# Paired 64-row scores, stacked parts for the banded heads, and grouped matmuls in a two-network kernel on Trainium2

## The chip, the cores and the metric

One Trainium2 chip (trn2), one core of it. The metric is the device time of one execution in microseconds, the median of the runs shown. TensorE (PE) does all matmuls and transposes, PEld are its weight loads; VectorE (DVE), ScalarE (ACT) and GpSimd (POOL) do the elementwise work, SP issues all DMAs.

## The reference, cut to what matters

Two small networks in a row, each of two layers, on 512 tokens of width 1024, all in float32. Every layer is a mixer (attention and other branches), in the first network also attention to a memory, and a gated feed-forward network. The attention parts that the change touches:

```python
# first network, both layers: 12 heads of 64 in 3 groups of dilation (1, 4, 16), causal
sc = jnp.einsum("bhqd,bhqkd->bhqk", qb[g], kk) * scale      # masked outside the window
o = softmax(sc) @ vv                                        # groups merged by their log sums
# second network, layer 0, "A": 8 banded heads over 2 key heads, band of 128, 256 context keys, a sink
p_loc, p_ctx, _ = joint_softmax(s_loc, s_ctx, s_sink)
# second network, layer 0, "B": 4 heads with two maps each, 512 + 256 keys
o = (softmax(q1 @ k1) - lam * softmax(q2 @ k2)) @ v
# second network, layer 1: latent attention, 16 heads of 64 + 32, 512 + 256 keys
```

## The kernel before, in words

Tokens stand in four tiles of 128 (two more for the 256 context tokens). Weights come from memory in units of up to 128 x 1024 (`wload`, line 124): SP loads `raw` (three buffers), ScalarE writes the high part `whi` (line 109), VectorE the low part `wlo` (line 112), five buffers of each. A product of two such split operands takes three matmuls: high by high, high by low, low by high (`mm3`, lines 134 to 138). Scores and projections are done that way; transposes, the products of probabilities with values and the small dilated scores are plain float32.

The attention of a mixer is a list of items, one per query tile and head, each with four steps: `qk` (scores into the PSUM tile S, two buffers of two banks, and the row minimum of the negated scores on VectorE), `soft` (exponential on ScalarE, scaling on GpSimd), `tr` (transposes through the PSUM tile T, copied back by ScalarE and VectorE as PT), `pv` (products with the values into p). `pipeline` (line 382) records the steps of different items interleaved, and after each turn some further work out of a list (`fill`): the next projection, the convolution or the pooling branch, in steps that each tell a length in ns.

Heads are 64 wide, so scores use 64 rows of the array: head or map 0 has partitions 0 to 63, head 1 has 64 to 127 (`rows` in `items1`, `diff_items`, `window_items`). `pv_pair` (line 439) puts two heads into the two column halves in turn. The stretches are the first network's mixer in both layers (`items1`, 32 items), the second network's first mixer (`diff_items`: 32 items and 8 of context; `window_items`: 32 banded items and 8 of context), and its second (`mla_items`, 96 rows, which uses `pv_pair` too).

The order on each engine is not what is written. A framework records the instructions and orders them by its own reckoning of when each could start, allots the buffers and sets semaphores; each engine then runs its list strictly in order. Names in the lists: a semaphore `DVE_49`, `Activation_49`, `Pool_49`, `PE_49` counts what that engine has finished, `DMAHW0_49` to `DMAHW7_49` count landed loads, `PE_sequencer_49` what TensorE's sequencer has passed.

Of the kernel before, what the change touches and what calls it, by code (L numbers as in the profile page):

```python
# [21 lines left out]
P = 128  # L22
S = 512
# [55 lines left out]
class Net:  # L79
# [398 lines left out]
    def items1(self, p, g, fill, oT):  # L478

        mm = self.nc.tensor.matmul  # L480
        sh = {}
        out = []

        def item(b, h):
            st = {}
            rows = slice(64 * h, 64 * h + 64)
            qs = slice(b * P, (b + 1) * P)

            def qk():
                if (b, h) == (0, 0):  # L490
                    fill.need(p)
                q0, k0, q12, k12 = g["q0"], g["k0"], g["q12"], g["k12"]
                ps = self.psum("S")
                self.mm3(ps[:, 0], (q0[rows, 0, qs], q0[rows, 1, qs]), (k0[rows, 0], k0[rows, 1]), True, True)
                for j in range(2):
                    o = ps[:, 1, j * P : (j + 1) * P]
                    mm(o, lhsT=q12[rows, j, qs], rhs=k12[rows, j, qs], start=True, stop=True)
                st["s"] = ps.rearrange("p a b -> p (a b)")[:, :768]
                st["nm"] = self.nmax(st["s"], mask=self.mask1[:, b])

            def soft():
                st["P"], r = self.exps(st["s"], st["nm"], 768)
                self.norm_probs(st["P"], r)

            def tr():
                sh[b, h] = self.probs_T(st["P"], 6)

            def pv():
                v = g["v"]
                o = self.psum("p")[:, :P]  # L510

                def vs(hh, k):
                    c = hh * 64 + (max(k - 3, 0)) * P
                    return v[:, k if k < 4 else b, c : c + 64]

                self.pv_pair(o, [sh[b, 0], sh[b, 1]], vs)
                self.copy(oT[:, qs], o)

            return (qk, soft, tr, pv if h else None)

        return [item(b, h) for b in range(4) for h in range(2)]
# [506 lines left out]

    def proj_ab(self, hT, i, g, tags, tiles=(0, 1, 2, 3, 4, 5)):
# [14 lines left out]
        lst = [("a", tok, 0, sc), ("b", tok, P, 1.0 if i < 4 else sc)] + ([("c", v, 0, 1.0)] if i == 4 else [])  # L1044
        for n, src, col, s in lst:
            g[n] = self.qk.tile([P, 2, 768], R, name="qk")
            yield from self.transposed(src, col, (4, 5), g[n], s, tag=tags[0])
            yield from self.transposed(src, col, range(4), g[n], s, tag=tags[-1])
        g["v"] = v

    def diff_items(self, h, g, fill, oB):
# [20 lines left out]
        def item(t, m, first):  # L1072
            st = {}
            rows = slice(64 * m, 64 * m + 64)
            q = slice(t * P, (t + 1) * P)

            def qk():
                if first:
                    fill.need(h)
                qT, kT = g["a"], g["b"]  # L1080
                ql = (qT[rows, 0, q], qT[rows, 1, q])
# [3 lines left out]
                st["s"] = ps.rearrange("p a b -> p (a b)")[:, :768]  # L1085
                st["nm"] = self.nmax(st["s"])

            def soft():
                sh.setdefault(t, []).append(self.exps(st["s"], st["nm"], 768))
                if m:  # L1090
                    combine(t)
# [4 lines left out]
            return (qk, soft, tr if m else None, (lambda: finish(t, 6)) if m else None)  # L1096

        def ctx_item(t):
            st = {}
            q = slice(t * P, (t + 1) * P)  # L1100

            def qk():
                qT, kT = g["a"], g["b"]
                ps = self.psum("S")
                st["nm"] = nm = self.sm.tile([P, 2], F32, name="nm2")
                for m in range(2):
                    rows = slice(64 * m, 64 * m + 64)
                    self.mm3(ps[:, m, :256], (qT[rows, 0, q], qT[rows, 1, q]), (kT[rows, 0, 512:], kT[rows, 1, 512:]), True, True)
                nc.vector.tensor_reduce(nm, ps[:, :, :256], axis=AX.X, op=ALU.min)
                st["s"] = ps  # L1110

            def soft():
                sh[t] = [self.exps(st["s"][:, m, :256], st["nm"][:, m : m + 1], 256) for m in range(2)]
                combine(t)

            def tr():
                sh["T", t] = self.probs_T(sh[t][0][0], 2)

            return (qk, soft, tr, lambda: finish(t, 2))

        return [item(t, m, t == 0 and m == 0) for t in range(4) for m in range(2)] + [ctx_item(t) for t in (4, 5)]
# [11 lines left out]
    def window_items(self, g4, g5, fill, oB, oT):  # L1133
# [3 lines left out]

        def item(t, c, kv):
            st = {}
            rows = slice(64 * kv, 64 * kv + 64)  # L1140
# [6 lines left out]
            def qk():  # L1147
                qT, kT = qs(c), g4["c"]
                ql = (qT[rows, 0, q], qT[rows, 1, q])
                ps = self.psum("S")  # L1150
                c0 = 512 - nl * P
                self.mm3(ps[:, 0, c0:], ql, (kT[rows, 0, k0 * P : k1 * P], kT[rows, 1, k0 * P : k1 * P]), True, True)
                self.mm3(ps[:, 1, :256], ql, (kT[rows, 0, 512:], kT[rows, 1, 512:]), True, True)
# [21 lines left out]
        def ctx_item(t, half, kv):  # L1175
            st = {}
            rows = slice(64 * kv, 64 * kv + 64)
            q = slice(t * P, (t + 1) * P)

            def qk():  # L1180
                kT = g4["c"]
                ps = self.psum("S")
                st["s"] = ps[:, 0].rearrange("p (c k) -> p c k", c=2)
                for c in range(2):
                    qT = qs(2 * half + c)
                    self.mm3(st["s"][:, c], (qT[rows, 0, q], qT[rows, 1, q]), (kT[rows, 0, 512:], kT[rows, 1, 512:]), True, True)
# [41 lines left out]
    def mix_ab(self, hT, lead):  # L1228
        nc, I = self.nc, self.I
        with ExitStack() as ctx:  # L1230
            with ExitStack() as c2:
# [25 lines left out]
                for i in range(1, 6):  # L1257
                    fill.add(i, self.proj_ab(hT, i, gs[i], ("p",)))
                items = []
                for h in range(4):  # L1260
                    items += self.diff_items(h, gs[h], fill, oB[h])
                n, oT = len(items), []
                items += self.window_items(gs[4], gs[5], fill, oB, oT)
                self.pipeline(items, fill, [3000] * n + [200] * (len(items) - n), (0, 1, 4, 5))
# [447 lines left out]
```

## Time and profile before

| | |
|---|---|
| median of 3 runs | 3590.36 us (3587.81 to 3595.63) |
| the profiled execution | 3594.31 us |
| its span, first to last instruction | 3592.5 us |
| TensorE busy | 3519.9 us, 98% |
| mean granted TensorE clock | 0.994 of full speed |

The profile is of one execution. Matmul durations overlap, since a matmul streams in while the one before it drains: what a matmul costs is the distance between starts. "x2" behind a row is two instructions merged. Plain float32 matmuls show as two records each.

### The profile page before, as it was taken

What the parts mean: (1) busy time and instruction counts of PE and PEld (TensorE: products, weight loads), DVE (VectorE), ACT (ScalarE), POOL (GpSimd) and SP (SyncE); (2) the same over time, 40 slices, a digit from 0 to 9 for tenths busy, and PEclk for the clock granted to TensorE, in tenths of its full rate; (3) what the DMA queues carried; (4) which work ended last, traced back from release to release, by engine and by line L of the source; (5) the groups of instructions that cost most, each with busy time, mean ns of one, the idle gap of its engine ahead of it and who ended that gap; (6) DMA issues with size and microseconds to landing.
All of it is one profiled execution on the core that took longest, in us unless ns stands there. A gap on an engine that the chain in (4) does not pass through costs nothing.

```text
span 3592.5 us, 48260 instructions
## 1 busy us (share of the span) xinstructions
PE 3519.9 (98%) x19261; PEld 2994.1 (83%) x19261; DVE 1917.2 (53%) x3018; ACT 1335.5 (37%) x2372; POOL 429.1 (12%) x572
## 2 busy tenths in 40 slices
PE   8999999999999999999999999999999989999998
PEld 8877798888898778888878887888888878888887
DVE  4453357466534335666766666536663466753243
ACT  4432344332443324532344446332111356643222
POOL 0211111000102111200011122200000122220001
PEclk9999999999999999999999999999999999999999
DMA  4233334344322433354431112335443121022232
GB/s 129 83 129 94 100 112 141 106 144 135 103 66 93 135 94 124 121 167 150 131 107 40 36 48 77 125 93 168 132 132 103 46 80 33 25 89 87 90 102 86
DMA packets 110130, 364.02 MB, mean 101 GB/s; under 512 B 16617, under 2 KB 18209, under 8 KB 109905
## 3 DMA queue, kind: packets, MB, share of 16 engines
q1 hardware_dynamic: 109904, 360.94, 31.7%
q8 instruction: 151, 2.47, 0.3%
q14 instruction: 75, 0.61, 0.1%
HBM read 347.16 MB, written 13.73 MB: 100 GB/s over the span
## 4 chain that ended last, share of the span: by engine, by line
PE 90%; DVE 3%; ACT 2%; POOL 2%; DMA 1%; issue 1%; SPq 0%; ACTq 0%; POOLq 0%; DVEq 0%
PE ps L136 21%; PE ps L137 21%; PE ps L138 21%; PE p L136 4%; PE p L137 4%; PE p L138 4%; PE T L430 3%; PE p L444 3%; PE S L136 2%; PE S L137 1%; PE S L138 1%; DMA adaw<-in_ada_w_dram 1%; PE T L138 1%; PE T L136 1%; PE T L137 1%
## 5 line engine op out<-in xcount | busy, mean ns | idle before, releaser
L112 DVE TENSOR_TENSOR wlo<-raw,whi 128x1024 fp32r<-128x1024 f32 (+2 forms) x510 | 603.8, 1190 | 734.6 <-ACT whi L109 719.3
L109 ACT ACTIVATE whi<-raw 128x1024 fp32r<-128x1024 f32 (+2 forms) x510 | 518.1, 1019 | 1113.1 <-PE ps L137 710.2
L137 PE MATMUL ps<-hTlo,whi 128*128 128x512 f32 (+1 forms) x2048 | 757.6, 370 | 4.1 <-DVE hTlo L177 4.0
L136 PE MATMUL ps<-hThi,whi 128*128 128x512 f32 (+1 forms) x2048 | 757.7, 371 | 2.7 <-ACT hThi L109 1.4
L138 PE MATMUL ps<-hThi,wlo 128*128 128x512 f32 (+1 forms) x2048 | 756.7, 370 | 0.0
L136 PEld LDWEIGHTS ps<-hThi,whi 128*128 128x128 f32 x2048 | 385.8, 189 | 73.0 <-issue 3.5
L137 PEld LDWEIGHTS ps<-hTlo,whi 128*128 128x128 f32 x2048 | 386.5, 189 | 69.9 <-DVE hTlo L177 4.5
L138 PEld LDWEIGHTS ps<-hThi,wlo 128*128 128x128 f32 x2048 | 386.3, 189 | 65.2
L930 DVE SCALAR_TENSOR_TENSOR acc<-adaw,cs,acc 128x1024 f32<-128x1024 f32 x168 | 209.4, 1279 | 14.6 <-DMA adaw<-in_ada_w_dram 14.3
L136 PE MATMUL ps<-whi,a 128*128 128x512 f32 x440 | 170.9, 392 | 0.7 <-ACT a L109 0.7
L138 PE MATMUL ps<-whi,a 128*128 128x512 f32 x440 | 170.6, 390 | 0.0
L137 PE MATMUL ps<-wlo,a 128*128 128x512 f32 x440 | 170.6, 390 | 0.0
L136 PE MATMUL p<-whi,hThi 128*128 128x384 f32 x464 | 163.1, 352 | 7.5 <-ACT hThi L175 3.1
L137 PE MATMUL p<-wlo,hThi 128*128 128x384 f32 x464 | 158.2, 341 | 4.7 <-DVE wlo L112 4.7
L154 POOL TENSOR_SCALAR rstd<-ms 128x1 f32<-128x1 f32 x78 | 24.1, 309 | 1137.9 <-ACT junk L152 1122.7
L138 PE MATMUL p<-whi,hTlo 128*128 128x384 f32 x464 | 158.2, 341 | 0.7 <-DVE hTlo L112 0.7
L262 DVE TENSOR_TENSOR y<-y,ps 128x1024 f32<-128x1024 f32 x88 | 106.6, 1218 | 85.7 <-PE ps L138 85.4
L136 PE MATMUL ps<-whi,act 128*128 128x512 f32 x352 | 138.2, 395 | 0.0
L137 PE MATMUL ps<-wlo,act 128*128 128x512 f32 x352 | 137.2, 392 | 0.0
L138 PE MATMUL ps<-whi,act 128*128 128x512 f32 x352 | 136.3, 390 | 0.0
L420 POOL TENSOR_SCALAR g<-g,den 128x768 f32<-128x768 f32 (+3 forms) x88 | 74.6, 850 | 424.3 <-DVE den L416 375.6
L109 ACT ACTIVATE PT<-T 128x384 f32<-128x384 f32 (+2 forms) x160 | 74.4, 465 | 111.6 <-PE T L430 109.6
(407 smaller groups left out, 6830.8 us busy)
## 6 DMA issues: line engine op xcount, KB each, us to landing
raw<-in_ffn_w_dram SPq DMA_DIRECT2D x132, 512.0 KB
adaw<-in_ada_w_dram SPq DMA_DIRECT2D x96, 512.0 KB
raw<-in_w_up_dram SPq DMA_DIRECT2D x88, 512.0 KB
raw<-in_w_gate_dram SPq DMA_DIRECT2D x48, 512.0 KB
raw<-in_w_down_dram SPq DMA_DIRECT2D x44, 512.0 KB
raw<-in_w_qkv_dram SPq DMA_DIRECT2D x48, 384.0 KB
xd<-x SPq DMA_DIRECT2D x20, 512.0 KB
raw<-in_w_conv_dram SPq DMA_DIRECT2D x18, 512.0 KB
```

The source lines that it names most:

```text
L109: return self.nc.scalar.activation(out, in_, AF.Copy, scale=scale)
L112: return self.nc.vector.tensor_tensor(out, a, b, op=ALU.subtract)
L136: mm(ps, lhsT=l[0], rhs=r[0], start=first, stop=False)
L137: mm(ps, lhsT=l[0], rhs=r[1], start=False, stop=False)
L138: mm(ps, lhsT=l[1], rhs=r[0], start=False, stop=last)
L154: nc.gpsimd.tensor_scalar(r, ms, 1.0, EPS, op0=ALU.mult, op1=ALU.add)
L262: self.nc.vector.tensor_tensor(yps[t], yps[t], y, op=ALU.add)
L420: self.nc.gpsimd.tensor_scalar(Pt, Pt, r, 1.0, op0=ALU.mult, op1=ALU.mult)
L430: nc.tensor.transpose(ps[:, k * P : (k + 1) * P], Pt[:, (k0 + k) * P : (k0 + k + 1) * P], self.ident)
L444: self.nc.tensor.matmul(o[64 * h : 64 * h + 64], lhsT=vs(h, k), rhs=PTs[h][:, k], start=k == 0, stop=k == nk - 1)
L930: nc.vector.scalar_tensor_tensor(acc[r], w, c, acc[r], op0=ALU.mult, op1=ALU.add)
```

## The change

Scores of two heads (or two maps) are one item now, with both S buffers: `mm3_two` issues each of the three products for head 0 and head 1 in turn. For the banded heads, `stacked` puts the high part of the queries on a head's own 64 partitions and the low part on the other 64, and `keys_twice` puts the same keys on both; two matmuls of 128 rows then give the three products and the low by low one. The grouped scores, and all products with the values, stand in `tc.tile_critical()`, which makes a group one unit for the framework's order. The turns (`steps`), the fill lengths and the order of the fill work differ too.

```diff
+    def mm3_two(self, pss, ls, rs):
+
+        for i, j in ((0, 0), (0, 1), (1, 0)):
+            for ps, l, r in zip(pss, ls, rs):
+                self.nc.tensor.matmul(ps, lhsT=l[i], rhs=r[j], start=(i, j) == (0, 0), stop=i == 1)
...
     def pipeline(self, items, fill, ns, steps=(0, 1, 2, 3)):
-        for i in range(len(items) + steps[-1]):
+
+        own = [it[4] if len(it) > 4 else steps for it in items]
+        for i in range(max(j + o[3] for j, o in enumerate(own)) + 1):
             for s in (0, 2, 1, 3):
-                j = i - steps[s]
-                if 0 <= j < len(items) and items[j][s] is not None:
-                    items[j][s]()
+                for j, it in enumerate(items):
+                    if j + own[j][s] == i and it[s] is not None:
+                        it[s]()
...
     def pv_pair(self, o, PTs, vs):
 
         nk = PTs[0].shape[1]
-        for k in range(nk):
-            for h in range(2):
-                self.nc.tensor.matmul(o[64 * h : 64 * h + 64], lhsT=vs(h, k), rhs=PTs[h][:, k], start=k == 0, stop=k == nk - 1)
+        with self.tc.tile_critical():
+            for k in range(nk):
+                for h in range(2):
+                    self.nc.tensor.matmul(o[64 * h : 64 * h + 64], lhsT=vs(h, k), rhs=PTs[h][:, k], start=k == 0, stop=k == nk - 1)
...
-    def items1(self, p, g, fill, oT):
+    def items1(self, p, g, proj, oT):
...
             def qk():
-                if (b, h) == (0, 0):
-                    fill.need(p)
+                if b == 0 and p:
+                    drain(proj)
                 q0, k0, q12, k12 = g["q0"], g["k0"], g["q12"], g["k12"]
-                ps = self.psum("S")
-                self.mm3(ps[:, 0], (q0[rows, 0, qs], q0[rows, 1, qs]), (k0[rows, 0], k0[rows, 1]), True, True)
-                for j in range(2):
-                    o = ps[:, 1, j * P : (j + 1) * P]
-                    mm(o, lhsT=q12[rows, j, qs], rhs=k12[rows, j, qs], start=True, stop=True)
-                st["s"] = ps.rearrange("p a b -> p (a b)")[:, :768]
-                st["nm"] = self.nmax(st["s"], mask=self.mask1[:, b])
+                pss = [self.psum("S") for _ in both]
+                with self.tc.tile_critical():
+                    self.mm3_two([ps[:, 0] for ps in pss], [(q0[r, 0, qs], q0[r, 1, qs]) for r in both], [(k0[r, 0], k0[r, 1]) for r in both])
+                    for j in range(2):
+                        for ps, r in zip(pss, both):
+                            mm(ps[:, 1, j * P : (j + 1) * P], lhsT=q12[r, j, qs], rhs=k12[r, j, qs], start=True, stop=True)
+                st["s"] = [ps.rearrange("p a b -> p (a b)")[:, :768] for ps in pss]
+                st["nm"] = [self.nmax(s, mask=self.mask1[:, b]) for s in st["s"]]
...
-                fill.add(1, self.proj1(l, 1, hT, gs[1], ("p",)))
+                proj = self.proj1(l, 1, hT, gs[1], ("p",))
+                fill.add("conv", self.conv_branch(l, hT, bF))
                 fill.add("pool", self.pool_in(l, hT, pooled))
-                fill.add("conv", self.conv_branch(l, hT, bF))
                 fill.add("pool", self.pool_out(l, pooled, aF))
-                self.pipeline(self.items1(0, gs[0], fill, oF[0]) + self.items1(1, gs[1], fill, oF[1]), fill, 7200, (0, 1, 2, 3))
+                items = self.items1(0, gs[0], None, oF[0]) + self.items1(1, gs[1], proj, oF[1])
+                self.pipeline(items, fill, [9000] * 4 + [8500] * 4, (0, 0, 1, 2))
...
+    def stacked(self, tok, col, tiles, dst, scale, tag):
...
+        for h in range(2):
+            own, other = slice(64 * h, 64 * h + 64), slice(64 - 64 * h, 128 - 64 * h)
+            self.copy(dst[own, h, c], ps[own], scale=scale)
+            self.nc.vector.scalar_tensor_tensor(dst[other, h, c], ps[own], scale, f32(dst[own, h, c]), op0=ALU.mult, op1=ALU.subtract)
...
+    def keys_twice(self, g):
...
+            for kv, k in enumerate(ks):
+                own, other = slice(64 * kv, 64 * kv + 64), slice(64 - 64 * kv, 128 - 64 * kv)
+                self.split(k[own, 0, c], k[own, 1, c], ps[own])
+                self.copy(k[other, 0, c], ps[own])
+                self.sub(k[other, 1, c], ps[own], f32(k[own, 0, c]))
...
-                ps = self.psum("S")
-                self.mm3(ps[:, 0], ql, (kT[rows, 0, :512], kT[rows, 1, :512]), True, True)
-                self.mm3(ps[:, 1, :256], ql, (kT[rows, 0, 512:], kT[rows, 1, 512:]), True, True)
...
+                with self.tc.tile_critical():
+                    for j, c, n in ((0, slice(0, 512), 512), (1, slice(512, 768), 256)):
+                        self.mm3_two([ps[:, j, :n] for ps in pss], ql, [(kT[r, 0, c], kT[r, 1, c]) for r in both])
...
+        def scores(ps, c, kv, q, keys):
+
+            k = g4["k", kv]
+            for i in range(2):
+                self.nc.tensor.matmul(ps, lhsT=qs(c)[:, kv, q], rhs=k[:, i, keys], start=i == 0, stop=i == 1)
```

TensorE's list at the first scores of the first network. Before:

```order
L137 MATMUL p<-wlo,hThi 128x384
L138 MATMUL p<-whi,hTlo 128x384
L136 MATMUL S<-qk 128x512
L137 MATMUL S<-qk 128x512
L138 MATMUL S<-qk 128x512
L497 MATMUL S<-qk 128x128 x2
L136 MATMUL p<-whi,hThi 128x384 [waits Activation_49]
```

After the change, at the same place:

```order
L138 MATMUL p<-whi,hTlo 128x384
L503 NO_OP [waits DVE_49,Activation_49]
L136 MATMUL p<-hThi,whi 128x512 [waits Activation_49]
L1761 UNCONDITIONAL_BRANCH [waits DMAHW2_49,DMAHW1_49,DMAHW3_49,DMAHW0_49,DMAHW4_49,PE_sequencer_49,DMAHW5_49,DVE_49,DMAHW6_49,PE_49,DMAHW7_49,Activation_49,Pool_49]
L144 MATMUL S<-qk 128x512 x6
L507 MATMUL S<-qk 128x128 x4
L503 UNCONDITIONAL_BRANCH
L137 MATMUL p<-hTlo,whi 128x512 [waits PE_49]
L503 NO_OP [waits PE_sequencer_49]
L138 MATMUL p<-hThi,wlo 128x512 [waits DVE_49]
```

Both heads' scores (L144, L507) are together now, behind a row that waits for thirteen semaphores, and the convolution's matmuls (L136 to L138 with 512 columns) lie around them where the projection's did.

SP's list of the same mixer, from the projections' weights on. Before:

```order
L129 DMA raw<-in_w_qkv_dram 128x768 x16
L129 DMA raw<-in_w_pool_dram 128x1024 x3
L129 DMA raw<-in_w_conv_dram 128x1024 x9
L129 DMA raw<-in_pool_w_dram 128x896
L129 DMA raw<-in_w_abc_dram 128x1024
```

After the change; each branch row marks where a unit of TensorE's lies in the common order, and itself waits for nothing:

```order
L129 DMA raw<-in_w_qkv_dram 128x768 x4
L129 DMA raw<-in_w_conv_dram 128x1024 x5
L1761 UNCONDITIONAL_BRANCH
L129 DMA raw<-in_w_conv_dram 128x1024 x2
L129 DMA raw<-in_w_qkv_dram 128x768 x2
L1761 UNCONDITIONAL_BRANCH
L129 DMA raw<-in_w_qkv_dram 128x768 x2
L1761 UNCONDITIONAL_BRANCH x2
L129 DMA raw<-in_w_qkv_dram 128x768
L1761 UNCONDITIONAL_BRANCH
```

Seven of the nine loads for the convolution come ahead of the twelve for the second projection, and the units lie between the loads.

TensorE's list in the last mixer, from the transposes of a second head on (L430, L438 the transposes, L444, L453 the products with values). Before:

```order
L430 MATMUL T<-ident,big 128x128 [waits DVE_49]
L430 MATMUL T<-ident,big 128x128 x2
L444 MATMUL p<-PT,v 64x128 x12
L136 MATMUL S<-kThi_23729,hClo 128x512 [waits Activation_49]
L137 MATMUL S<-kTlo_23730,hClo 128x512
```

After the change, at the corresponding place:

```order
L438 MATMUL T<-ident,big 128x128 x2
L450 NO_OP [waits PE_sequencer_49,DVE_49,Activation_49]
L136 MATMUL S<-kThi_23820,hChi 128x512 [waits Activation_49]
L1761 UNCONDITIONAL_BRANCH [waits DMAHW2_49,DMAHW1_49,DMAHW3_49,DMAHW0_49,DMAHW4_49,PE_sequencer_49,DMAHW5_49,DVE_49,DMAHW6_49,PE_49,DMAHW7_49,Activation_49,Pool_49]
L453 MATMUL p<-PT,v 64x128 x12
L450 UNCONDITIONAL_BRANCH
L137 MATMUL S<-kTlo_23821,hChi 128x512 [waits PE_49]
L450 NO_OP [waits PE_sequencer_49]
L138 MATMUL S<-kThi_23820,hChi 128x512
```

The twelve products stood between transposes and scores with no wait of their own; now a wait for all semaphores stands ahead of them, and they lie inside the next head's three score passes. The whole list has 104 such rows: 36 ahead of scores and 68 ahead of products.

## Rows read from the trace of the kernel before

**Rows 1.** Page, part 1: busy time, share of the span, instructions of each engine
```profile
PE 3519.9 (98%) x19261; PEld 2994.1 (83%) x19261; DVE 1917.2 (53%) x3018; ACT 1335.5 (37%) x2372; POOL 429.1 (12%) x572
```

**Rows 2.** Page, part 4: shares of the chain that ended last, by engine
```profile
PE 90%; DVE 3%; ACT 2%; POOL 2%; DMA 1%; issue 1%; SPq 0%; ACTq 0%; POOLq 0%; DVEq 0%
```

**Rows 3.** Stretches: length, busy us of PE, PEld, DVE, ACT, POOL; clock, DMA share, GB/s
```profile
72.80:250.20 177.40, 174.66 (x1023) 148.72 (x1022) 79.79 (x159) 69.55 (x119) 32.13 (x44) 0.99 0.29 92
998.50:1175.50 177.00, 174.55 (x1022) 148.43 (x1021) 78.56 (x158) 69.18 (x116) 31.32 (x40) 0.99 0.28 89
1903.30:2142.00 238.70, 234.08 (x1407) 207.56 (x1408) 151.11 (x378) 99.20 (x257) 41.76 (x75) 1.00 0.13 43
2142.00:2231.00 89.00, 87.78 (x716) 67.97 (x716) 63.78 (x244) 59.63 (x190) 29.52 (x46) 1.00 0.06 16
2949.70:3173.00 223.30, 221.42 (x1896) 194.74 (x1896) 156.60 (x330) 145.34 (x313) 60.03 (x64) 1.00 0.11 33
```

**Rows 4.** Timeline, TensorE, first scores of the kernel: start us, duration us, line
```profile
72.60 0.34 PE L138 MATMUL p<-whi,hTlo 128*128 128x384 f32 x1
72.87 0.50 PE L136 MATMUL S<-qk 64*128 64x512 f32 x1
73.21 0.39 PE L137 MATMUL S<-qk 64*128 64x512 f32 x1
73.44 0.39 PE L138 MATMUL S<-qk 64*128 64x512 f32 x1
73.67 0.60 PE L497 MATMUL S<-qk 64*128 64x128 f32 x4
74.20 0.45 PE L136 MATMUL p<-whi,hThi 128*128 128x384 f32 x1
74.49 0.34 PE L137 MATMUL p<-wlo,hThi 128*128 128x384 f32 x1
74.66 0.33 PE L138 MATMUL p<-whi,hTlo 128*128 128x384 f32 x1
```

**Rows 5.** Timeline, TensorE, two context score groups that met
```profile
2128.66 0.39 PE L136 MATMUL S<-qk 64*128 64x256 f32 x2
2128.89 0.29 PE L137 MATMUL S<-qk 64*128 64x256 f32 x2
2129.01 0.29 PE L138 MATMUL S<-qk 64*128 64x256 f32 x2
2129.14 0.28 PE L136 MATMUL S<-qk 64*128 64x256 f32 x1
2129.26 0.28 PE L137 MATMUL S<-qk 64*128 64x256 f32 x1
```

**Rows 6.** Groups by line: busy us, mean ns of one, idle before and releasers
```profile
L399 DVE TENSOR_REDUCE nm<-S 128x1 f32<-128x768 f32 x96 | 91.4, 952 | 44.3 <-PE S L138 43.8
L411 ACT ACTIVATE g<-S,nm 128x768 f32<-128x768 f32 x64 | 57.7, 901 | 26.1 <-DVE nm L399 17.8 <-DVE nm L401 6.2 <-POOL t L578 1.4
L420 POOL TENSOR_SCALAR g<-g,den 128x768 f32<-128x768 f32 x56 | 54.2, 968 | 354.9 <-DVE den L416 324.7 <-issue 22.1 <-PE p L444 5.5
```

**Rows 7.** Timeline, SP queue and ScalarE, around the same first scores
```profile
71.72 2.41 SPq L129 DMA_DIRECT2D raw<-in_w_qkv_dram  x3
...
74.86 0.85 ACT L109 ACTIVATE whi<-raw 128x768 fp32r<-128x768 f32 x1 [1.39 <-DMA raw<-in_w_qkv_dram]
```

**Rows 8.** Busy time by stretch, two of 6 us ahead of the last mixer; columns as rows 3
```profile
2925.00:2931.00 6.00, 2.75 (x21) 2.23 (x19) 5.01 (x8) 3.79 (x8) 1.34 (x3) 1.00 0.58 186
2931.00:2937.00 6.00, 3.49 (x11) 3.52 (x12) 1.50 (x2) 1.03 (x2) 2.93 (x4) 0.53 0.13 36
```

**Rows 9.** Instructions of line 444: the one semaphore instruction on the TensorE queue
```profile
L444 PEldq EVENT_SEMAPHORE  x1: 51/51/51, 2229.3 to 2229.3; - x1
```

**Rows 10.** Waits of ScalarE: us in total, times, longest
```profile
ACT whi L109 <- PE ps L137: 710.2, 213, 7.1
```

More of the change, by code (lines that the diff above doesn't have):

```diff
@@ L514, in vs @@
                     return v[:, k if k < 4 else b, c : c + 64]
[L516 removed]
+                self.pv_pair(o, sh[b], vs)
                 self.copy(oT[:, qs], o)
[L519 to L521 removed]
+            return (qk, soft, tr, pv)
+        return [item(b) for b in range(4)]
     def shifts(self, dst, src, k):
@@ L1043, in proj_ab, with diff_items @@
         sc = -(64 ** -0.5)
-        lst = [("a", tok, 0, sc), ("b", tok, P, 1.0 if i < 4 else sc)] + ([("c", v, 0, 1.0)] if i == 4 else [])
+        lst = [("a", tok, 0, sc), ("b", tok, P, 1.0 if i < 4 else sc)]
         for n, src, col, s in lst:
             g[n] = self.qk.tile([P, 2, 768], R, name="qk")
-            yield from self.transposed(src, col, (4, 5), g[n], s, tag=tags[0])
-            yield from self.transposed(src, col, range(4), g[n], s, tag=tags[-1])
+            to = self.transposed if i < 4 else self.stacked
+            yield from to(src, col, (4, 5), g[n], s, tag=tags[0])
+            yield from to(src, col, range(4), g[n], s, tag=tags[-1])
         g["v"] = v
-    def diff_items(self, h, g, fill, oB):
+    def keys_twice(self, g):
+        ks = (self.qk.tile([P, 2, 768], R, name="qk"),
+              self.work.tile([P, 6, 256], R, name="tok").rearrange("p a b -> p (a b)").rearrange("p (a b) -> p a b", a=2))
+        for tiles in ((4, 5), range(4)):
+            n = len(tiles) * P
+            yield 0.0
+            ps = self.psum("p")[:, :n]
+            for j, t in enumerate(tiles):
+                self.nc.tensor.transpose(ps[:, j * P : (j + 1) * P], g["v"][:, t], self.ident)
+                yield 109
+            c = slice(tiles[0] * P, tiles[0] * P + n)
+            for kv, k in enumerate(ks):
[3 more added lines that the diff above has]
+                self.sub(k[other, 1, c], ps[own], f32(k[own, 0, c]))
+        g["k", 0], g["k", 1] = ks
+    def diff_items(self, h, g, fill, oB, after):
         nc = self.nc
@@ L1070, in finish, with item, tr @@
             nc.vector.scalar_tensor_tensor(oB[:, t], o, r, self.subln, op0=ALU.mult, op1=ALU.mult)
-        def item(t, m, first):
+        def item(t):
             st = {}
-            rows = slice(64 * m, 64 * m + 64)
+            both = [slice(0, 64), slice(64, 128)]
             q = slice(t * P, (t + 1) * P)
             def qk():
-                if first:
+                if t == 0:
                     fill.need(h)
+                    fill.add(*after)
                 qT, kT = g["a"], g["b"]
-                ql = (qT[rows, 0, q], qT[rows, 1, q])
-                ps = self.psum("S")
-                self.mm3(ps[:, 0], ql, (kT[rows, 0, :512], kT[rows, 1, :512]), True, True)
-                self.mm3(ps[:, 1, :256], ql, (kT[rows, 0, 512:], kT[rows, 1, 512:]), True, True)
-                st["s"] = ps.rearrange("p a b -> p (a b)")[:, :768]
-                st["nm"] = self.nmax(st["s"])
-            def soft():
-                sh.setdefault(t, []).append(self.exps(st["s"], st["nm"], 768))
-                if m:
+                ql = [(qT[r, 0, q], qT[r, 1, q]) for r in both]
+                pss = [self.psum("S") for _ in both]
+                with self.tc.tile_critical():
+                    for j, c, n in ((0, slice(0, 512), 512), (1, slice(512, 768), 256)):
+                        self.mm3_two([ps[:, j, :n] for ps in pss], ql, [(kT[r, 0, c], kT[r, 1, c]) for r in both])
+                st["s"] = [ps.rearrange("p a b -> p (a b)")[:, :768] for ps in pss]
+                st["nm"] = [self.nmax(s) for s in st["s"]]
+            def soft():
+                sh[t] = [self.exps(s, nm, 768) for s, nm in zip(st["s"], st["nm"])]
+                combine(t)
+            def tr():
+                sh["T", t] = self.probs_T(sh[t][0][0], 6)
+            return (qk, soft, tr, lambda: finish(t, 6), (0, 0, 2, 3))
@@ new lines, in ctx_item, with qk, soft @@
+        def ctx_item():
+            st = {}
+            def qk():
+                qT, kT = g["a"], g["b"]
+                both = [slice(0, 64), slice(64, 128)]
+                for t in (4, 5):
+                    st[t] = self.psum("S"), self.sm.tile([P, 2], F32, name="nm2")
+                with self.tc.tile_critical():
+                    for t in (4, 5):
+                        q = slice(t * P, (t + 1) * P)
+                        self.mm3_two([st[t][0][:, m, :256] for m in range(2)], [(qT[r, 0, q], qT[r, 1, q]) for r in both],
+                                     [(kT[r, 0, 512:], kT[r, 1, 512:]) for r in both])
+                for ps, nm in st.values():
+                    nc.vector.tensor_reduce(nm, ps[:, :, :256], axis=AX.X, op=ALU.min)
+            def soft():
+                for t, (ps, nm) in st.items():
+                    sh[t] = [self.exps(ps[:, m, :256], nm[:, m : m + 1], 256) for m in range(2)]
@@ L1091, in soft @@
                     combine(t)
             def tr():
-                sh["T", t] = self.probs_T(sh[t][0][0], 6)
[L1096 to L1119, printed above, removed]
@@ L1121, in diff_items @@
-        return [item(t, m, t == 0 and m == 0) for t in range(4) for m in range(2)] + [ctx_item(t) for t in (4, 5)]
+                for t in st:
+                    sh["T", t] = self.probs_T(sh[t][0][0], 2)
+            return (qk, soft, tr, lambda: [finish(t, 2) for t in st], (0, 0, 2, 3))
+        return [item(t) for t in range(4)] + [ctx_item()]
     def diff_T(self, oB, oT):
@@ L1184, in qk @@
                 for c in range(2):
-                    qT = qs(2 * half + c)
-                    self.mm3(st["s"][:, c], (qT[rows, 0, q], qT[rows, 1, q]), (kT[rows, 0, 512:], kT[rows, 1, 512:]), True, True)
+                    scores(st["s"][:, c], 2 * half + c, kv, q, slice(512, 768))
             def soft():
@@ L1256, in mix_ab, with last @@
                 oB = [oBp.tile([P, 6, P], F32, name=f"oB{h}") for h in range(4)]
-                for i in range(1, 6):
-                    fill.add(i, self.proj_ab(hT, i, gs[i], ("p",)))
+                proj = [(i, self.proj_ab(hT, i, gs[i], ("p",))) for i in range(1, 6)]
                 items = []
                 for h in range(4):
-                    items += self.diff_items(h, gs[h], fill, oB[h])
+                    items += self.diff_items(h, gs[h], fill, oB[h], proj[h])
+                qk5 = items[-1][0]
+                def last():
+                    qk5()
+                    fill.add(*proj[4])
+                    fill.add(5, self.keys_twice(gs[4]))
+                items[-1] = (last,) + items[-1][1:]
                 n, oT = len(items), []
                 items += self.window_items(gs[4], gs[5], fill, oB, oT)
-                self.pipeline(items, fill, [3000] * n + [200] * (len(items) - n), (0, 1, 4, 5))
+                self.pipeline(items, fill, [6000] * 20 + [200] * (len(items) - n), (0, 1, 4, 5))
                 fill.drain()
```

30 lines of the change are left out of this document (18 added, 12 removed).

## The prediction

> **What bounds the kernel now.** First the page's busy shares: TensorE is busy 3519.9 of 3592.5 us [rows 1], so it idles 73 us in all. Second the chain that ended last: 90% of it is TensorE, every other engine 3% or less [rows 2]. Third the stretches in which attention is computed, five of them, 905 us together [rows 3]: in each TensorE is busy 98 to 99% of the time, VectorE 44 to 72%. So a step removed from TensorE's queue there is worth its full length, and a stop put into that queue costs its full length. Fourth the timeline, for what one step costs. Steps are read from start to start, since the durations overlap.
>
> **What the change takes off TensorE.** *Passes.* In [rows 4] a 64-row pass of 512 columns starts 0.23 us after the one before it, and the four short passes of line 497 take 0.60 us with a last one of some 0.27, so 0.11 each. One head of the first mixer is 3 x 0.23 + 4 x 0.11 = 1.13 us. Are two row halves as quick as one? The old order brought three couples together by chance ("x2") [rows 5]: couple follows couple after 0.12 us, and the single passes behind them follow each other after 0.12 us as well. A couple costs what a single costs. So 16 pairs in the first mixer (2 layers, 2 projections, 4 blocks) give 16 x 1.13 = 18 us; 16 pairs of the two-map heads (3 x 0.23 + 3 x 0.12 = 1.05 each) 17 us; their 8 context tiles (3 x 0.12) 3 us. The banded heads go from 3 passes to 2: 32 items save one pass of 256 or 384 columns (0.12, or 0.17 as a projection pass in [rows 4]) and one of 256, 8 us; their context items 8 x 2 x 0.12 = 2 us. Sum 48 us; if 512-column couples did not overlap, 10.
>
> Rule against row: a couple adds about 0.01 us to a single in [rows 5]. The Trainium skill, "TensorE: Matmul & The Clock Gate", Part 3, "Measured speedup vs the span model", gives a four-fold row packing as 3.07 times; the same loss for two tiles would make 38 us of these savings about 26, and the total 12 us later. The couples of [rows 5] are this kernel's own, so I keep 48.
>
> *Changes of shape.* When TensorE goes from 128 to 64 rows in [rows 4], the first 64-row pass starts 0.27 us after the last projection pass in place of 0.17, and the next after 0.34 in place of 0.23; on the way back the projection's first step is 0.29 in place of 0.17. That is 0.2 us for one change, 0.1 if its second half is hidden. The built lists have 452 such changes before and 240 after, because grouped passes are no longer cut by projections and transposes and the banded scores are 128 rows high. 212 x 0.2 = 42 us (21 at least). Together TensorE's own work is 90 us shorter.
>
> **What it adds.** The built order is what I rest on. Each of the 104 grouped units (36 of scores, 68 of products with values, 32 of those in the last mixer, which has no other edit) stands behind a row that waits for thirteen semaphores. They are TensorE's own matmuls, ScalarE, VectorE, GpSimd, and all eight semaphores on which loads land; each value is that of the last instruction or load listed ahead of the unit, needed by it or not. Behind the unit the next matmuls stand behind a wait for TensorE's own semaphore, until it is empty. Nothing in the trace of before is such a stop, so each part of its cost is bounded.
>
> *Emptying.* The last matmul must end: 0.34 us in [rows 4] where the next began after 0.27. One semaphore instruction on TensorE's queue is 0.05 us [rows 9]. Behind the unit the same, and the next weights are not loaded ahead, 0.1 us more. I take 0.3 us for both ends, 31 us in all (bounds 0.15 and 0.6: 16 and 62).
>
> *Loads.* In 33 units the newest load stands at most 15 matmuls ahead, in 21 of them at most 5. Three loads issued from 71.72 let ScalarE go on at 74.86: the first landed 3.1 us after its issue [rows 7]. With 5 or fewer matmuls of 0.17 to 0.23 us gone, about 2.6 us are left, with 10 or so gone 1.1: 21 x 2.6 + 12 x 1.1 = 68 us. Below, nothing is left of it; above, 33 x 3.1 = 102. Until now such a load was covered by the projection's own matmuls; that cover is what the wait removes.
>
> *Other engines.* The other 71 units wait for the last instruction listed on VectorE, ScalarE or GpSimd; in 89 of the 104 one of them stands within 3 matmuls, so it has hardly begun. One is the row minimum at 0.95 us, the exponential at 0.90 or the scaling at 0.97 [rows 6]. I take one whole instruction, 71 x 0.95 = 67 us. Below, a third of one (22); above, minimum and exponential in a row (131).
>
> *Refilling.* While TensorE stands, the others run out of scores and transposes, so the next transposes wait for minimum, exponential and scaling, 2.8 us in a row [rows 6], as far as no projection covers it. Mostly one does: I take 0.3 us a unit, 31 us (0 to 62).
>
> *Clock.* In the 6 us to 2931 TensorE worked 2.75 us, and in the 6 us behind that its granted clock was 0.53, between the two levels 1.2 and 2.4 GHz but nearly the lower [rows 8]. Stops of 3 us may bring that on. Those 6 us lost at most 0.47 x 6 = 2.8 us of TensorE's work; I take half of that for one stop and six such stops, 10 us (0 to 35).
>
> *At no cost.* The stacked parts and doubled keys add 14 instructions each to ScalarE and VectorE, of 0.4 to 0.9 us; they lie in the stretch from 1903 to 2142, where VectorE is busy 151 of 239 us [rows 3]. If that cover failed, about 8 us. The first mixer's second projection is now run in one piece before its first pair, and the convolution branch fills the first half instead: the same matmuls and the same loads in another order on SP's queue, seven of the convolution's ahead of the projection's twelve. Its cost is in the loads above, since a wait on them is what the new order can hit. Queued behind a waiting TensorE are the projections, so all weight buffers are freed later, and SP's next loads with them.
>
> **The sum.** -48 - 42 + 31 + 68 + 67 + 31 + 10 = +117 us. The profiled execution took 3594.3 us, 1.8 around its span and 4 over the median of the runs shown: 3594 + 117 = **3711 us**.
>
> **Rivals.**
> 1. *The waits are met already* (faster). Then only the emptying is paid: 3594 - 90 + 31 = 3535 us. For it: ScalarE's weight splits spend 710 us waiting for TensorE [rows 10], so the others mostly stand ready. Against it: what they wait for is a buffer that TensorE has just freed, so split and load begin just then and are what the next unit must wait for. It decides if loads, engines, refilling and clock cost under 59 us, 0.57 a unit; up to 3590. Chance 0.07.
> 2. *Every wait is a long one.* Loads 102, engines 131, clock 35, the rest as above: 3594 - 90 + 31 + 102 + 131 + 31 + 35 = 3834 us. It needs the landing to be slower than in [rows 7], or two instructions in front of each unit. Chance 0.10.
> 3. *The readers of the scores set the pace.* A pair takes both score buffers, and the next pair waits for two minima and two exponentials, 3.7 us [rows 6]; then the 38 us of the pairs come to nothing: 3749. Against it, groups stand about 12 us apart (239 us for 16 pairs and 4 context groups [rows 3]). The Trainium skill, "TensorEngine Tiling (Array Packing)", "PSUM Bottleneck", says that tiling speeds up TensorE but not the reading of PSUM; by it this would be the case. Chance 0.05.
> 4. *512-column couples do not overlap*, so the change does not do what it says: the same 38 us, 3749. Chance 0.03.
>
> **How the numbers follow.** The forecast has 0.75. With loads and engines at a little over half, and no clock or refilling, it reaches down to 3630; with refilling, emptying and clock at their upper bounds (+87) less some of it, up to 3785. Rivals 3 and 4 lie inside; left out are rival 1, most of rival 2 and a little of the forecast. Slower by over 0.2% (7 us, about what a measurement of this kernel tells from no change): forecast, rivals 2 to 4, 0.93. Rival 1 splits into faster 0.05 and same 0.02.
>
> **What would show it.** Right: idle time of TensorE up from 73 to above 200 us, most of it just ahead of lines 144 and 453 and ended by DMA, VectorE and GpSimd; gaps of 2 us or more in some 20 places; the last mixer longer than its 223 us by 20 us or more, although only its products were grouped; couples of L144 0.23 us apart. Wrong: idle time ahead of those lines under 0.5 us a unit (rival 1), or couples 0.46 us apart (rival 4), or idle time ahead of L144 that ends with the exponential of the pair before (rival 3).

## The result, and the profile after the change

The change takes 3802.85 us (median of 4 runs, 3794.18 to 3811.33), the kernel before 3590.69 us beside it: ratio 1.0589, 95% interval 1.0563 to 1.0616, 212 us slower. Forecast were 3711 us (3630 to 3785). The direction was right, the size was not: the time lies 92 us above the forecast and 18 us above its range.

The profiled execution took 3802.17 us, its span is 3800.4 us, 207.9 more than before. Part 1 of its page, busy time and instructions of each engine (against [rows 1]):

```profile
PE 3528.9 (93%) x19181; PEld 2997.9 (79%) x19181; DVE 1926.3 (51%) x3032; ACT 1339.9 (35%) x2386; POOL 426.8 (11%) x572
```

TensorE idles 3800.4 - 3528.9 = 271.5 us, in place of 72.6: 199 more. And it is busy 9 us longer, with fewer passes. The attention stretches, columns as [rows 3] (length, busy us of PE, PEld, DVE, ACT, POOL, then clock, DMA share, GB/s):

```profile
74.80:286.70 211.90, 175.16 (x1020) 146.65 (x1020) 78.38 (x158) 66.90 (x116) 31.83 (x42) 0.93 0.22 71
1038.90:1260.20 221.30, 185.53 (x1020) 155.72 (x1020) 77.39 (x157) 67.03 (x115) 30.55 (x40) 0.87 0.21 66
1993.80:2283.00 289.20, 230.01 (x1379) 208.26 (x1379) 159.07 (x386) 104.39 (x267) 39.90 (x75) 0.90 0.10 33
2283.00:2389.60 106.60, 76.21 (x652) 57.84 (x652) 63.53 (x246) 58.59 (x190) 29.81 (x46) 0.97 0.05 16
3108.40:3380.20 271.80, 230.60 (x1896) 199.60 (x1896) 151.77 (x327) 142.83 (x310) 60.24 (x64) 0.97 0.07 23
```

They grew by 34.5, 44.3, 50.5, 17.6 and 48.5 us: 195 of the 208. The last mixer, where only the products were grouped, grew by 48.5 over 32 units. The column on the right of the busy times is the surprise: [rows 3] show a clock of 0.99 to 1.00, here it is 0.87 to 0.97.

Where TensorE stood, by line (busy us, mean ns; then idle just before, and what ended it):

```profile
L453 PE MATMUL p<-PT,v 128*64 128x128 f32 (+1 forms) x1088 | 77.0, 291 | 55.1 <-DMA raw<-in_mla_w_out_dram 8.2 <-DVE nm L411 7.3 <-ACT PT L109 7.3
L144 PE MATMUL S<-qk 64*128 64x512 f32 (+1 forms) x336 | 49.5, 428 | 68.8 <-DMA raw<-in_ab_w_in_dram 15.8 <-issue 13.4 <-ACT qk L109 8.4
L453 PE MATMUL p<-PT,vt 128*64 128x128 f32 x384 | 34.1, 346 | 19.7 <-DVE nm L409 5.9 <-POOL t L591 5.0 <-ACT whi L109 3.4
L438 PE MATMUL T<-ident,g 128*128 128x128 f32 x440 | 79.5, 295 | 20.4 <-ACT PT L109 5.2 <-DVE PT L441 4.8 <-DVE den L1110 4.2
```

143.6 us stand right ahead of the 104 units (L144, L453). Summed over the view of waits, a load ended 51 us of it (16 units), VectorE, ScalarE or GpSimd 68 us (70 units), the rest (24 us, 18 units) TensorE itself or nothing that the profile shows. One such place, on SP's queue and TensorE:

```profile
2028.49 2.41 SPq L129 DMA_DIRECT2D raw<-in_ab_w_in_dram  x3
...
2029.55 0.27 PE L438 MATMUL T<-ident,g 128*128 128x128 f32 x1
...
2034.26 1.65 PE L144 MATMUL S<-qk 64*128 64x256 f32 x12 [4.45 <-DMA raw<-in_ab_w_in_dram]
```

Three loads for a later projection are issued from 2028.49 on; the scores behind them use none of them, and TensorE stands 4.45 us until the last has landed. The cheapest entry into a unit shows what is left when nothing is late:

```profile
2009.33 0.34 PE L138 MATMUL p<-whi,hTlo 128*128 128x384 f32 x1
2009.52 0.27 PE L438 MATMUL T<-ident,big 128*128 128x128 f32 x1
2010.21 1.32 PE L144 MATMUL S<-qk 64*128 64x512 f32 x12 [0.43 <-ACT tok L109]
2011.62 0.76 PE L438 MATMUL T<-ident,big 128*128 128x128 f32 x5
```

From the last matmul to the unit's first pass 0.70 us; behind its last pass the next start comes after 0.36 us, about the least behind 96 of the 104 units (behind the other 8 it is 0.20). The instructions between are now in the trace (line by line: count, then shortest, middle and longest duration in ns):

```profile
L1761 PEldq EVENT_SEMAPHORE  x626: 51/51/6122, 68.4 to 3800.3; - x157
L1761 PEldq COMPARE_BRANCH  x104: 163/163/309, 74.5 to 3378.5; - x104
```

Six semaphore instructions for each unit, 0.106 us from start to start, and a branch of 0.16. The same rows, not merged, show that the couples work: twelve passes (six of 512 columns, six of 256) start within 1.04 us, two of a couple 0.003 to 0.01 us apart; singly they would take 3 x 0.23 + 3 x 0.12 = 1.05 for one map alone [rows 4, 5].

### The profile page after: what moved, and what is told of

Same layout as the page of the kernel before. It is cut to its first block, busy times and chain, and to the rows that moved or that the text cites. A ratio compares the mean times of both kernels' runs of the same rounds, so it can differ in the third digit from the quotient of the medians.

```text
span 3800.4 us, 49456 instructions
## 1 busy us (share of the span) xinstructions
PE 3528.9 (93%) x19181; PEld 2997.9 (79%) x19181; DVE 1926.3 (51%) x3032; ACT 1339.9 (35%) x2386; POOL 426.8 (11%) x572
## 5 line engine op out<-in xcount | busy, mean ns | idle before, releaser
L136 PE MATMUL ps<-hThi,whi 128*128 128x512 f32 (+1 forms) x2048 | 757.8, 371 | 3.0 <-ACT hThi L109 1.4
L138 PE MATMUL ps<-hThi,wlo 128*128 128x512 f32 (+1 forms) x2048 | 756.7, 370 | 0.0
L136 PEld LDWEIGHTS ps<-hThi,whi 128*128 128x128 f32 x2048 | 386.1, 189 | 73.8 <-issue 3.4
L138 PEld LDWEIGHTS ps<-hThi,wlo 128*128 128x128 f32 x2048 | 386.5, 189 | 65.3
L944 DVE SCALAR_TENSOR_TENSOR acc<-adaw,cs,acc 128x1024 f32<-128x1024 f32 x168 | 209.4, 1278 | 14.7 <-DMA adaw<-in_ada_w_dram 14.6
L136 PE MATMUL ps<-whi,a 128*128 128x512 f32 x440 | 170.9, 392 | 0.6 <-ACT a L109 0.6
L136 PE MATMUL p<-whi,hThi 128*128 128x384 f32 x464 | 163.9, 353 | 8.0 <-ACT hThi L181 3.1
L138 PE MATMUL ps<-whi,a 128*128 128x512 f32 x440 | 170.6, 390 | 0.0
L138 PE MATMUL p<-whi,hTlo 128*128 128x384 f32 x464 | 160.8, 346 | 0.9 <-DVE hTlo L112 0.8
L136 PE MATMUL ps<-whi,act 128*128 128x512 f32 x352 | 138.2, 394 | 0.0
L138 PE MATMUL ps<-whi,act 128*128 128x512 f32 x352 | 136.2, 390 | 0.0
L407 DVE TENSOR_REDUCE nm<-S 128x1 f32<-128x768 f32 x96 | 90.6, 951 | 79.2 <-PE S L138 39.5
```

Source lines behind the costliest of these rows:

```text
L407: self.nc.vector.tensor_reduce(nm, sv, axis=AX.X, op=ALU.min)
L944: nc.vector.scalar_tensor_tensor(acc[r], w, c, acc[r], op0=ALU.mult, op1=ALU.add)
```

## The experiments

Two theories at the start. **U**: the units cost it, by their waits, restarts and the clock. **O**: the new order costs it (pairs that take both score buffers, two heads' softmax at once, the moved projection).

### With and without units

e1_no_units: the four blocks are plain code.

```diff
-        with self.tc.tile_critical():
-            for k in range(nk):
+        for k in range(nk):
...
-                with self.tc.tile_critical():
-                    self.mm3_two(
+                self.mm3_two(
...
```

> The change with its pairs, stacked parts, order of steps and order of loads, but no group is a unit for the scheduler (the four tile_critical blocks are plain code). In its built order 20 of the 32 groups of 512 columns still stand together, the others are cut once or twice. Theory U (the units cost it: the waits ahead of them, the restart behind them and the low clock they bring): the savings of the prediction remain, 90 us less some 20 for cut groups and what the other engines then miss, so 3590 - 70 = about 3520 us (3500 to 3560), TensorE idle back under 100 us, mean granted clock 0.99 or more. Theory O (the new order costs it: pairs that take both score buffers, softmax steps of two heads at once, the projection moved ahead): it stays near the change, 3700 to 3800 us, with the idle time ahead of the scores and transposes.

Measured 3611.34 us (1.0055, 1.0038 to 1.0072): neither theory's number. 3803 - 3611 = 192 us are the units, 1.84 us each, so U holds for the loss. But the 90 us of savings aren't there either; without units the change is still 21 us slower than before.

```profile
71.60:256.30 184.70, 171.94 (x1023) 144.73 (x1022) 78.97 (x160) 68.56 (x120) 30.10 (x42) 0.95 0.28 86
1921.80:2172.00 250.20, 223.95 (x1372) 201.29 (x1373) 157.32 (x380) 101.64 (x259) 38.95 (x69) 0.94 0.13 41
2172.00:2255.00 83.00, 81.19 (x672) 62.34 (x670) 65.51 (x258) 61.69 (x199) 32.11 (x51) 1.00 0.07 20
2972.40:3195.60 223.20, 221.37 (x1896) 194.75 (x1896) 156.58 (x330) 145.00 (x314) 59.78 (x64) 1.00 0.11 33
```

The last mixer is back at 223.2 us: there the units were the whole loss. The banded heads went from 89 to 83 us, so the stacked parts earn 6. The first mixer (184.7 for 177.4) and the two-map heads (250.2 for 238.7) are longer than before with less TensorE work: TensorE idles 13 and 26 us there, and the clock is at 0.95 and 0.94. That part is O.

e2_score_units: the change with units around the 36 groups of scores, none around products (its edit is the first piece of the diff above).

> The change with units around the 36 groups of scores only; the 68 groups of products are plain code again. In the trace of the change the starts ahead of the products' units take 98 us and those behind them 29 us, of which some 27 us would pass in any case, so 100 us are the products' units, and some 20 us of low clock. Theory U: 3803 - 120 = about 3680 us (3640 to 3720). Theory O: 3780 us or more, since the score groups and their order are as they were.

Measured 3702.41 us (1.0313, 1.0298 to 1.0328), inside U's range: 100 us for the 68 units of products, 91 for the 36 of scores, 1.5 and 2.5 us each.

e3_product_units: the kernel before, and one edit.

```diff
-        for k in range(nk):
-            for h in range(2):
+        with self.tc.tile_critical():
+            for k in range(nk):
+                for h in range(2):
```

> The kernel before, its only edit a unit around each of the 68 groups of products (no pairs, no stacked parts, loads and steps as before). The last mixer, where the change has no other edit, grew by 48.6 us over 32 units, 1.5 us each. Theory U: 68 x 1.5 = 103, so about 3695 us (3660 to 3730). Theory O: the same within 20 us (3590 to 3610).

Measured 3753.51 us (1.0447, 1.0414 to 1.0479): 164 us, 2.4 a unit. Theory O is out for this part, and U's 103 us were too few. The banded heads' stretch tells why; before it has 716 matmuls, 87.78 us busy, at a clock of 1.00 [rows 3], now:

```profile
2198.00:2350.00 152.00, 131.16 (x711) 99.53 (x710) 61.54 (x240) 58.97 (x184) 28.70 (x45) 0.61 0.04 11
```

The same passes take 131.16 us: 43 of the 63 us more in this stretch are busy time at a granted clock of 0.61; the other 20 are idle time, 20.8 us in place of 1.2 for 20 units. Cut where the clock falls, the stretch is:

```profile
2198.00:2232.00 34.00, 28.10 (x219) 21.66 (x218) 21.52 (x79) 19.69 (x55) 8.55 (x12) 1.00 0.01 1
2232.10:2350.00 117.90, 103.06 (x492) 77.87 (x492) 39.92 (x162) 39.29 (x129) 20.15 (x33) 0.50 0.04 14
```

The longest stop of TensorE in the 34 us before the fall, and at it, is 1.13 us. This is one execution; the four of e3 take 3734 to 3762 us, with mean clocks of 0.980 to 0.970 in the same order.

e4_product_units_halved: the same with every unit cut into two, so 136.

```diff
-        with self.tc.tile_critical():
-            for k in range(nk):
+        for ks in (range(nk // 2), range(nk // 2, nk)):
+            with self.tc.tile_critical():
+                for k in ks:
```

> As the run with product units alone, but each of the 68 groups is cut into two units, so there are 136. The second of two has little new to wait for: it measures what a unit costs by its own instructions. Theory U1 (a fixed part of its own: in the trace of the change six semaphore instructions stand 0.106 us apart ahead of a unit, then a branch of 0.16, and the shortest distance from the last matmul to a unit's first is 0.70 us; behind a unit the next start comes after 0.36): 68 x some 0.9 = 61 us more than the run with 68 units. Theory U2 (a unit costs only by the loads and engines it waits for): 68 x 0.3 = 20 us more. Theory U3 (every unit waits anew for something just begun): 68 x 1.5 = 100 us more.

Measured 3891.63 us, 138 more than with 68 units, above all three. Counted apart over the trace, TensorE idles 91.0 us ahead of the first halves (91.5 ahead of the whole groups in e3) and 41.5 us ahead of the second, 0.6 each; from the pass before a second half to its first pass it is 69 us in all, 1.0 each. That agrees with U1. In all the idle time is 218.3 us against 171.8, so 47 of the 138 us. The rest is busy time, 3671.3 us for 3588.7 with the same matmuls: the part of it at the lower level of the clock (1.2 GHz) rises from 185 to 308 us, counted over the trace. A pass of 512 columns starts 0.43 us after the one before it there, in place of 0.23, so this costs some 123 / 2 = 61 us at most. So the clock is a large part of what such a unit costs, but under half.

### The order of the fill work

e5_old_order: no units, pairs and stacked parts kept, the fill work in the order of before in both mixers.

```diff
-                proj = self.proj1(l, 1, hT, gs[1], ("p",))
-                fill.add("conv", self.conv_branch(l, hT, bF))
+                fill.add(1, self.proj1(l, 1, hT, gs[1], ("p",)))
                 fill.add("pool", self.pool_in(l, hT, pooled))
+                fill.add("conv", self.conv_branch(l, hT, bF))
...
-                self.pipeline(items, fill, [9000] * 4 + [8500] * 4, (0, 0, 1, 2))
+                self.pipeline(items, fill, 10500, (0, 0, 1, 2))
...
-                    fill.add(*after)
...
-            return (qk, soft, tr, lambda: finish(t, 6), (0, 0, 2, 3))
+            return (qk, soft, tr, lambda: finish(t, 6), (0, 1, 3, 4))
...
+                for pr in proj[:4]:
+                    fill.add(*pr)
```

> The run without units took 21 us more than the kernel before although its score passes and the entries into them take some 60 us less. Here it gets the order of the fill work of before in both mixers: the first mixer's second projection, the pooling branch and the convolution in one list (10500 ns a turn), and in the second network's first mixer all projections in the list from the start, with softmax, transposes and products one turn later (0, 1, 3, 4). Theory O1 (the new order of fill work lets TensorE run dry at the places where one head's work ends, and the clock falls there): the 42 us of added idle time and the 22 us of added low clock go, and what is left of the savings shows: 3611 - 45 = about 3566 us (3550 to 3585). Theory O2 (pairs as such cost it, because two heads' softmax and transposes now come at once): about 3600 us, no better than before.

e6_old_order_first and e7_old_order_second: the pieces for one mixer alone.

> The run without units, the old order of fill work in the first network's mixer alone (the two stretches that are 7.3 and 8.8 us longer than before in the run without units). Theory O1: both stretches fall back to 177 us or some 5 less, 3611 - 22 = about 3589 us. Theory O2: 3605 us or more.

> The run without units, all projections in the list from the start and the steps one turn apart in the second network's first mixer alone (250.2 us there in place of 238.7). Theory O1: that stretch falls to some 230 us, 3611 - 20 = about 3591 us. Theory O2: 3605 us or more.

e8_pairs_second_only: as e5, with the first network's mixer wholly that of before.

> As the run with the old order in both mixers, but the first network's mixer is that of before, single heads and all; pairs and stacked parts in the second network alone, no units. Tells what the pairs of the first mixer earn: 18 us of passes by the prediction's sum, so by theory O1 this is 10 to 18 us slower than the run with the old order in both, about 3580 us; by theory O2 it is faster than that run.

Measured: e5 3581.25 us (0.9971, 0.9958 to 0.9983), e6 3588.64, e7 3603.52, e8 3585.91. O1 holds for the first mixer (e6: 23 us less than e1, as expected); in the second the old order gives back 8 us, near O2's end. e5 is 9 us faster than the kernel before and the fastest of all kernels here, but at the far end of its range. Part 1 of its page:

```profile
PE 3484.9 (97%) x19181; PEld 2963.1 (83%) x19181; DVE 1924.9 (54%) x3032; ACT 1337.6 (37%) x2386; POOL 427.0 (12%) x572
```

TensorE has 35 us less to do than before, and idles 98.9 us in place of 72.6. The largest group of that idle time is transposes that wait for their predecessors' copies:

```profile
PE T L438 <- ACT PT L109: 12.7, 14, 3.1
```

Two heads' transposes now stand one behind the other, with two T buffers; that this is the reason is read from the code and was not tried. The pairs of the first mixer earn some 5 us (e8 against e5; the times of the two, 3581 to 3592 and 3579 to 3586 us, overlap), not the 18 of their passes. With these pairs TensorE is busy 14.6 us less (3484.9 for 3499.5) and idles 9.8 us more (98.9 for 89.1), so most of what they save is waited away even without units.

### Units again, and the clock

e9_units_old_order: e5 with all 104 units (the four lines of `tile_critical` of the change).

> All 104 units of the change, with the old order of the fill work in both mixers (the run with the old order, 3581 us, plus units). Theory U: units add what they added to the order of the change, 3803 - 3611 = 192 us, so 3581 + 192 = about 3773 us (3745 to 3800). Rival: the units cost so much only because of the change's order of loads (seven of the convolution's ahead of the projection's twelve); then here 3581 + 140 = about 3720 us or less.

Measured 3770.43 us (1.0498, 1.0480 to 1.0515): 189 us for the same 104 units, as expected. The rival, that only this order of loads made the units dear, is out.

e10_clock_filled: e3 with useless passes behind each unit of the banded heads (the lines stand in two places, for the token and for the context items); they add work and leave nothing out. e11_filled_control: the same passes in the kernel before.

```diff
                 self.pv_pair(o, [sh[t, c, 0], sh[t, c, 1]], vs)
+                extra = self.psum("p")
+                for _ in range(10):
+                    self.nc.tensor.matmul(extra, lhsT=g4["a"][:, 0, q], rhs=g4["c"][:, 0, :512], start=True, stop=True)
```

> The run with product units alone (3754 us), and in the banded heads' stretch (152 us there in place of 89, at a mean granted clock far under 1) behind each of the 20 units ten more 128-row passes of 512 columns, whose result nobody reads (extra work, 20 x 10 x 0.23 = 46 us at the high level). Theory C (TensorE stands so often there that the clock is at its lower level, and that costs some 37 us of the 63): with the extra passes the clock stays high for longer, so the extra work is paid in part by the higher clock and by the waits it fills: 10 to 25 us more than the run without it, and the granted clock of the stretch above 0.9. Theory W (it is the waits alone, the clock is only their shadow): 40 us or more on top, 3795 us.

> The kernel before with the same 200 extra passes at the same places and no units: what the extra passes cost where TensorE never stands. Both theories: 46 us, so about 3637 us (3630 to 3645).

Measured: e11 3636.13 us, 45.5 more than before, as expected; e10 3760.28, 6.8 more than e3, which is within the spread of e3's own runs; the stretch tells more. In e10:

```profile
2205.40:2358.50 153.10, 135.62 (x903) 101.81 (x903) 64.61 (x240) 59.16 (x185) 28.83 (x45) 0.98 0.04 11
```

and in e11:

```profile
2142.00:2275.00 133.00, 132.76 (x909) 102.25 (x909) 64.64 (x244) 59.98 (x188) 29.43 (x45) 1.00 0.06 19
```

In e10 there are 20 units and 45 us of extra work, and the stretch is 1.1 us longer than in e3. TensorE idles 17.5 us in place of 20.8, so it was not the waits that were filled: the clock is 0.98 in place of 0.61, and the passes take 135.62 us, 2.9 more than in the control, where they took 43 too many in e3. Theory C holds, more strongly than expected: in this stretch the clock is a cost of its own beside the waits.

## Why the prediction was wrong, point by point

The sum was -48 - 42 + 31 + 68 + 67 + 31 + 10 = +117; the profile shows +208.

**Passes, -48, and changes of shape, -42.** Couples and stacked parts do what the prediction said, so rival 4 is out. The Trainium skill, "TensorE: Matmul & The Clock Gate", Part 3, "Measured speedup vs the span model", gives 3.07 times for four tiles; the same loss for two, which would have made 26 of the pairs' 38 us, is not seen here: their passes start together and follow each other as single ones do. For the sum of both terms the runs without units speak. In e5 TensorE is busy 35 us less than before; 54 us of its busy time fall where the clock is at the lower level of 1.2 GHz, against 32 before (counted over the trace), which costs up to (54 - 32) / 2 = 11 us; so passes and shapes together are -46. In e1 it is -19 - (89 - 32) / 2 = -47. The 48 of the passes account for that, so nothing is left for the shapes. Their changes fell at the scores (266 with a 64-row side before, 106 in e1) but rose around the products (166 to 228), which now meet other shapes oftener, and one costs 0.1 us rather than 0.2: a product behind a transpose starts after 0.20 us in place of 0.11. In the change itself the count fell as the built list said (414 to 202 over the trace), but the stops stand where the changes were. The step that failed is "212 x 0.2 = 42 us".

**Emptying, loads, other engines and refilling, 31 + 68 + 67 + 31 = 197.** The idle time rose by 199, near the sum, and rival 1, for which these had to cost under 59, is out. But that the sum comes out is luck in part: only 271.5 - 114.3 = 157 us of the rise are the units (e1 idles 114.3 us). The parts were not as written. Emptying is dearer than its upper bound of 0.6 a unit: at the cheapest entry, with the usual way out, (0.70 - 0.20) + (0.36 - 0.20) = 0.66 us against a start with a change of shape, an estimate of 69 us for 104. The row of a single semaphore instruction [rows 9] was taken for all of it; there are six, further apart than they are long, and a branch. The waits for loads (51 us) and engines (68 us) include part of this, so they were smaller than written. And e1 idles 42 us more than before with no unit at all, the rest of the 199, which the prediction had at nothing ("the same matmuls and the same loads in another order").

**Clock, 10 (0 to 35).** This is the largest miss, and the other step that failed. 169 us of TensorE's busy time are at the lower level, 32 before, so it costs at most 137 / 2 = 69 us; and if passes and shapes are -47 as in e1, 208 - 199 + 47 = 56. [Rows 8] were read as six stops of 3 us that bring the clock down for a while; in e3 it fell after stops of no more than 1.13 us and stayed down to the end of the stretch, 118 us. The first units of the two layers show it on the same six passes, the second at the lower level (clock 0.50 from 1038.5 to 1045.3 us):

```profile
74.83 0.96 PE L144 MATMUL S<-qk 64*128 64x512 f32 x6 [3.13 <-DMA raw<-in_w_conv_dram]
...
1038.92 1.65 PE L144 MATMUL S<-qk 64*128 64x512 f32 x6 [3.56 <-DMA raw<-in_w_conv_dram]
```

So the 208 - 117 = 91 us missing are 46 to 59 of clock, 43 to 30 of savings on shapes that weren't there, and 2 of idle time. How clock and shapes divide within these bounds is open. The forecast's own small sums are loose too, without weight here: half of 2.8 us six times is 8, not 10, and loads and engines at a little over half give a lower end of some 3610, not 3630.

**What would show it.** Idle time above 200 us, ahead of lines 144 and 453, ended by loads, VectorE, ScalarE and GpSimd; gaps of 2 us or more in some 20 places (22 ahead of units); the last mixer 48.5 us longer: all as forecast. Rival 2 (3834 us, every wait long) comes nearest in time and is not what happened: loads and engines are no more than forecast. Rival 3 is out for the units: loads end half of the idle time ahead of L144 (34.7 of 68.8 us) and the exponential of the pair before ends none of it, and e6 and e5 take the pairs without loss against the kernel before.

## What to carry to other kernels

A block that the scheduler may not cut can become a barrier: it waits for everything listed ahead of it, needed or not. Price it by its fixed instructions, by what has just begun (a load, an exponential), and by the clock that the stops bring down. Here a unit cost 1.8 us; by an estimate from the change against e1 (157 us of idle time, (169 - 89) / 2 = 40 us of clock, over 104 units) the three parts are about 0.7, 0.8 and 0.4 us. Before giving up a grouping that saves passes, try it without the barrier and with the old order of the work around it: that turned +212 us into -9.

## What was not expected of the hardware

The time that TensorE stood does not tell the clock in these runs. In e3's banded stretch it was busy 131 of 152 us and had a granted clock of 0.61; in the change's own banded stretch it was busy 76 of 107 us, with stops of up to 2.46 us, and had 0.97. The scores are passes of 64 rows in the first and of 128 in the second, and their number and order differ too; which of these the clock goes by was not tried, so why e10's extra passes kept it high is open. Two 64-row passes of 512 columns on the two halves of the array cost no more than one (0.003 to 0.01 us apart).
